# Last quad's down projection: two output blocks by token parts of 320 and 192, instead of one block by halves

## The chip, the core and the metric

The kernel runs on one core of one Trainium2 chip. The metric is the device time of one execution in microseconds (us): the median of 3 runs. Engines: TensorE (PE in the profile, PEld for its weight loads), VectorE (DVE), ScalarE (ACT), GpSimd (POOL) and SyncE (SP, which here only issues transfers).

## The reference

One block of a two-stream backbone over 512 latent tokens and 256 context tokens of width 2048: a mixing layer (gated linear attention and mLSTM heads), then a SwiGLU feed-forward layer with a depthwise 3x3 convolution on its gate branch, then the final norm. What the change touches is the end:

```python
h2 = rmsnorm(x, g_norm2) * (1 + sc2) + sh2
x = x + gt2 * conv_ffn(h2, rows, GRID_W, w_up, conv_w, conv_b, w_down)
...
return rmsnorm(x, g_final)
```

`conv_ffn` ends in a product of its 5504 hidden features with `w_down` (5504 x 2048). `rmsnorm` needs, for every token, the mean of the squares over all 2048 features, so no output of a token can be scaled before all 16 feature tiles of that token are done.

## The kernel before

**Layout.** Features lie on the 128 partitions and tokens along the free dimension. The residual stream is 16 tiles of 128 features x 512 tokens (`x2[k]`, tile name `xf` at the end). Matrix products are made in float32r, each operand split into a rounded part and its rest (`split`, L104: ScalarE casts, VectorE subtracts), and `mm3` (L120) issues three products per pair. Each product loads its own stationary weights.

**Stages.** Most of the time goes to the projections and the feed-forward layer. The hidden features are worked through in eleven quads (`QUADS`), each with `up_gate`, `convolve`, `up_val` and a down projection. The down projection of a quad has four output blocks of 512 features (four tiles each). For all quads but the last, `down_sums` adds each block to the residual stream in DRAM.

**The last quad** (L1339 to L1419) adds in SBUF instead. Blocks 0, 1 and 2 go through `down_block` (L1286): weights by `load_split`, then 48 products of 512 tokens into four PSUM banks (`dn`). Then, for each tile, VectorE adds the product to the residual (`residual`, L1084), ScalarE squares it by halves of 256 tokens (`square`, L1088; VectorE adds the squares up in `sqfq`), and ScalarE multiplies the tile by its column of g_final (L1365).

Block 3 is made by halves (`halves`, L1346) of 256 tokens, from weights that are split ahead of it (`dlh`, `dll`, L1369 to L1376), into banks `dl`. For each half, when its four tiles are done, `token_rstd` (L1104) makes the root: products of the squares with a column of ones give the sum per token (`ps_rmsf`), `mean_rsqrt` (L170) makes the root by two ScalarE and four VectorE steps (`rs_rmsf`), and products with the identity spread it over the partitions (`rb_rmsf`). `scaled` (L1377) then copies it for GpSimd (`r3s`), multiplies all 16 tiles of the half into output buffers (`o`, two tiles each), and issues eight transfers to DRAM per half. VectorE makes eleven of a half's 16 scalings and GpSimd five (L1389); tiles 12 to 15 take g_final in the same VectorE instruction (L1386).

**What sets the order.** While `pinned` is on (from L1395), TensorE keeps program order. The first half's sums are issued after the second half's first tile, its spread after the second tile, and its scalings then run on the other engines during the second half's last two tiles. The other engines' order is made by a scheduler at build time from data dependences and priorities (`tc.high_priority`); each engine then runs its list in order. PSUM has eight banks, `acc` and `psb` take them in turn.

Of the kernel before, what the change touches and what calls it, by code (L numbers as in the profile page):

```python
# [18 lines left out]
P = 128  # L19
# [4 lines left out]
T = 512  # L24
# [59 lines left out]
def block_kernel(ctx: ExitStack, tc: tile.TileContext, a: dict, out: bass.AP):  # L84
# [1019 lines left out]
    def token_rstd(sums, pl, name, n=T, idle=0):  # L1104

        nj = n // P
        ps = psb(f"ps_{name}", (P, nj))
        for i, sq in enumerate(sums):
            for j in range(nj):
                mm(ps[:, j : j + 1], sq[:, P * j : P * j + P], cst[:, C_ONE : C_ONE + 1],  # L1110
                   start=(i == 0 and j == 0), stop=(i == len(sums) - 1), skip_group_check=True)
        var, scr, r = (pl.tile([P, nj], F32, name=f"{t}_{name}", tag=t) for t in ("rs1", "rs2", "rs3"))
        with tc.high_priority():
            mean_rsqrt(ps, D, var, scr, r)
        yield
        o = psb(f"rb_{name}", (P, n))
        idle_products(o[:, 0:P], sums[0][:, 0:P], idle)
        for j in range(nj):
            mm(o[:, P * j : P * j + P], r[:, j : j + 1].to_broadcast([P, P]), ident, start=True, stop=True)
        yield o  # L1120
# [225 lines left out]
    halves = [slice(0, T // 2), slice(T // 2, T)]  # L1346
# [10 lines left out]
    for blk in range(3):  # L1357
        accs = down_block(q, blk)
        with tc.high_priority():
            for i in range(4):  # L1360
                residual(4 * blk + i, accs[i], modc[5])
        for k in range(4 * blk, 4 * blk + 4):
            for hf, sl in enumerate(halves):
                square(k, sums3[hf], sqp, f"fq{hf}", sl)
            S.activation(x2[k], x2[k], AF.Copy, scale=gnf[:, k : k + 1])  # L1365
        if blk == 0:
            for k in range(12, KT):
                nc.gpsimd.dma_start(x2[k], x2d[k])
    wd = []  # L1369
    for n, f in enumerate(fs):  # L1370
# [5 lines left out]
        wd.append((wh, wl))  # L1376
    def scaled(hf, sl, r3):  # L1377

        r3s = sqp.tile([P, T // 2], F32, name=f"r3s{hf}", tag=f"r3s{hf}")
        S.copy(r3s, r3)  # L1380
        for k in range(0, KT, 2):
            o = operand(k // 2, "l", "q", f"o{hf}_{k}", (P, 2, T // 2), F32)
            for i in range(2):
                xx = x2[k + i][:, sl]
                if k + i >= 12:
                    V.scalar_tensor_tensor(out=o[:, i, :], in0=xx, scalar=gnf[:, k + i : k + i + 1], in1=r3,  # L1386
                                           op0=ALU.mult, op1=ALU.mult)
                elif k in (2, 6) or k + i == 10:
# [3 lines left out]
            eng = nc.scalar if hf and k % 4 == 2 else nc.sync  # L1392
            eng.dma_start(out[k : k + 2, :, sl].rearrange("k p t -> p k t"), o)

    pinned[0] = True  # L1395
    root = None
    for hf, sl in enumerate(halves):
        accs = [acc(f"dl{hf}_{i}", (P, T // 2)) for i in range(4)]
        order = [(n, i) for n in range(len(fs)) for i in range(4)]
        if hf == 1:  # L1400
            order = [(n, i) for i in range(4) for n in range(len(fs))]
        for at, (n, i) in enumerate(order):
            if hf and at in (4, 8):
                with tc.high_priority():
                    r3 = next(root)
                    if at == 8:
                        scaled(0, halves[0], r3)
            gh, gl = gs[fs[n]]
            mm3(accs[i], wd[n][0][:, P * i : P * i + P], wd[n][1][:, P * i : P * i + P],
                gh[:, sl], gl[:, sl], n == 0, n == len(fs) - 1)  # L1410
        with tc.high_priority():
            for i in range(4):
                residual(12 + i, accs[i], modc[5], sl)
                square(12 + i, sums3[hf], sqp, f"fq{hf}", sl)
        root = token_rstd(sums3[hf], sqp, f"rmsf{hf}", T // 2, idle=4 * hf)
    with tc.high_priority():
        _, r3 = root
        scaled(1, halves[1], r3)
# [71 lines left out]
```

## Time and profile before

| | us |
|---|---|
| median of 3 runs | 2452.11 (2451.01 to 2452.73) |
| the profiled execution | 2453.06 |
| its span, first to last instruction | 2451.2 |
| TensorE busy | 2406.2 (98%) |
| VectorE busy | 1795.0 (73%) |
| ScalarE busy | 1003.7 (41%) |
| GpSimd busy | 176.5 (7%) |
| first product of block 2 | at 2412.57 |
| first product of block 3 | at 2423.45 |
| last product of block 3 ends its pace | at 2437.25 |
| second half's root spread over the partitions | at 2441.46 |

Times in the traces are us from the span's start. The profiled execution takes 1.86 us outside its span. The engines overlap, so busy shares don't add up; a stage is bound by what ends last in it, and the chain of waits follows that back from the last instruction. A matmul's duration in the rows includes the time in which its results drain from the array, beside the next one; the spacing of their starts is the pace.

### The profile page before, as it was taken

The numbers are of one execution on the slowest core, as the hardware profiler recorded it, in microseconds if no ns is written. First come the engines' busy times: TensorE is split into PE (matmuls) and PEld (weight loads), VectorE is DVE, ScalarE is ACT, GpSimd is POOL, SyncE is SP. The second block draws the span as 40 slices with busy tenths as digits, with TensorE's granted clock in tenths as the row PEclk, the third lists the DMA queues.
The fourth block names the chain that finished last, engine by engine and source line by source line (L and its number), as shares of the span: only waits on it lengthen the run. The fifth ranks groups of instructions, "written<-read, shape, count | busy, mean of one in ns | idle before, by whom it ended". The sixth has DMA issues, their size and how long they took to land.

```text
span 2451.2 us, 38648 instructions
## 1 busy us (share of the span) xinstructions
PE 2406.2 (98%) x15412; PEld 2170.5 (89%) x15412; DVE 1795.0 (73%) x2876; ACT 1003.7 (41%) x1494; POOL 176.5 (7%) x221
## 2 busy tenths in 40 slices
PE   6999999999999999999999999999999999999998
PEld 4887899899988888888998989999999999999997
DVE  6566856655456586769888787878787878787886
ACT  4225443222232242246544444444444444444445
POOL 0000000000000000000101010101111111111021
PEclk9999999999999999999999999999999999999999
DMA  9751111134355788843555455555555555546464
GB/s 383 286 173 55 46 44 52 61 112 129 129 181 187 245 301 283 282 148 112 126 144 143 130 139 137 136 140 129 139 135 140 128 145 124 147 123 148 117 185 133
DMA packets 122486, 373.65 MB, mean 152 GB/s; under 512 B 13912, under 2 KB 19010, under 8 KB 122306
## 3 DMA queue, kind: packets, MB, share of 16 engines
q1 hardware_dynamic: 95298, 318.75, 39.7%
q0 software_dynamic: 25920, 51.40, 11.6%
q8 instruction: 120, 1.97, 0.3%
q10 hardware_dynamic: 1088, 1.05, 0.1%
q14 instruction: 60, 0.49, 0.1%
HBM read 320.80 MB, written 50.34 MB: 151 GB/s over the span
## 4 chain that ended last, share of the span: by engine, by line
PE 88%; issue 6%; DVE 3%; DMA 2%; ACT 1%; POOL 0%; SPq 0%; DVEq 0%; POOLq 0%; ACTq 0%
PE a L111 19%; PE dn L111 17%; PE uv L111 16%; PE ug L111 15%; PE ga L111 7%; PE wo L111 7%; PE po L111 2%; PE ps_m L111 1%; PE sl L111 1%; DMA raw_m<-in_w_mod 1%; PE st L111 1%; PE cst L111 1%; DMA raw_uv<-in_w_up 0%; DVE ex L94 0%; DMA xl<-in_xT 0%
## 5 line engine op out<-in xcount | busy, mean ns | idle before, releaser
L111 PE MATMUL dn<-gh,lo_d 128*128 128x512 f32 x672 | 262.2, 390 | 1.6 <-DVE lo_d L106 1.6
L111 PE MATMUL dn<-gh,hi_d 128*128 128x512 f32 x672 | 261.6, 389 | 0.0
L111 PE MATMUL dn<-gl,hi_d 128*128 128x512 f32 x672 | 261.6, 389 | 0.0
L1257 DVE SCALAR_TENSOR_TENSOR cv<-pads,cwt,cv 128x512 f32<-128x512 f32 x344 | 239.3, 748 | 0.6
L1311 POOL DMA_DIRECT2D x2d<-st x160 | 140.1, 930 | 1143.5 <-ACT st L1310 1069.4
L106 DVE TENSOR_TENSOR lo_buv<-sum_uv,hi_buv 128x1024 fp32r<-128x1024 f32 x80 | 98.0, 1225 | 104.1 <-ACT hi_buv L105 101.4
L320 DVE SCALAR_TENSOR_TENSOR raw_m<-raw_m,crow 128x1024 f32<-128x1024 f32 x128 | 154.7, 1229 | 1.6 <-DMA raw_m<-in_w_mod 1.6
L111 PEld LDWEIGHTS dn<-gh,lo_d 128*128 128x128 f32 x672 | 126.1, 188 | 30.1 <-DVE lo_d L106 3.9
L111 PE MATMUL a<-hi_h,hTh 128*128 128x256 f32 x512 | 152.0, 297 | 0.5 <-ACT e L402 0.5
L111 PEld LDWEIGHTS dn<-gl,hi_d 128*128 128x128 f32 x672 | 126.2, 188 | 25.8
L111 PEld LDWEIGHTS dn<-gh,hi_d 128*128 128x128 f32 x672 | 126.2, 188 | 25.7
L111 PE MATMUL a<-lo_h,hTh 128*128 128x256 f32 x512 | 145.1, 283 | 0.0
L111 PE MATMUL a<-hi_h,hTl 128*128 128x256 f32 x512 | 144.9, 283 | 0.0
L105 ACT CAST hi_d<-raw_d 128x1024 fp32r<-128x1024 f32 x86 | 88.6, 1030 | 130.8 <-PE ug L111 70.6
L106 DVE TENSOR_TENSOR lo_d<-raw_d,hi_d 128x1024 fp32r<-128x1024 f32 x86 | 102.9, 1197 | 49.6 <-ACT hi_d L105 48.9
L111 PE MATMUL ug<-bth,hi_bug 128*128 128x256 f32 x480 | 136.8, 285 | 0.2 <-DVE t L1276 0.2
L111 PE MATMUL uv<-bth,lo_buv 128*128 128x256 f32 x480 | 135.9, 283 | 0.3 <-DVE lo_buv L106 0.3
L111 PE MATMUL ug<-bqh,lo_aug 128*128 128x256 f32 x480 | 135.8, 283 | 0.0
L111 PE MATMUL uv<-bqh,lo_auv 128*128 128x256 f32 x480 | 135.8, 283 | 0.0
L111 PE MATMUL uv<-bql,hi_auv 128*128 128x256 f32 x480 | 135.8, 283 | 0.0
L111 PE MATMUL ug<-bqh,hi_aug 128*128 128x256 f32 x480 | 135.8, 283 | 0.0
L111 PE MATMUL uv<-bth,hi_buv 128*128 128x256 f32 x480 | 135.8, 283 | 0.0
(410 smaller groups left out, 7255.4 us busy)
## 6 DMA issues: line engine op xcount, KB each, us to landing
raw_m<-in_w_mod SPq DMA_DIRECT2D x192, 512.0 KB, 5.2
raw_d<-in_w_down SPq DMA_DIRECT2D x82, 512.0 KB, 3.5
raw_ug<-in_w_up SPq DMA_DIRECT2D x80, 512.0 KB, 3.5
x2d<-st POOLq DMA_DIRECT2D x160, 256.0 KB, 5.5
raw_uv<-in_w_up SPq DMA_DIRECT2D x80, 512.0 KB, 5.7
raw_h<-in_w_heads SPq DMA_DIRECT2D x64, 512.0 KB, 3.5
raw_ga<-in_w_gates SPq DMA_DIRECT2D x32, 512.0 KB, 4.1
raw_wo<-in_w_out SPq DMA_DIRECT2D x32, 512.0 KB, 4.7
```

The lines of the kernel that those rows point to most:

```text
L105: cast[0] = S.copy(hi, x).ins
L106: return V.tensor_tensor(out=lo, in0=x, in1=hi.bitcast(F32), op=ALU.subtract).ins
L111: ins = PE.matmul(*args, **kw)
L320: V.scalar_tensor_tensor(out=x, in0=x, scalar=1.0, in1=crow[0], op0=ALU.mult, op1=ALU.mult, accum_out=mtot[:, at : at + 1])
L1257: V.scalar_tensor_tensor(out=t3, in0=src, scalar=w, in1=t3, op0=ALU.mult, op1=ALU.add)
L1311: nc.gpsimd.dma_start(x2d[k], t, accum_op=ALU.add)
```

## The change

- Blocks 2 and 3 of the last quad are both made by parts, and the parts are 320 and 192 tokens (`parts`) instead of halves of 256. Block 2 no longer goes through `down_block`; its weights are still loaded and split by `load_split` (two pairs of f, kept for both parts).
- A part runs block 2, then block 3. In the first part block 2 runs with f outermost, everything else with the output tile outermost. Each tile gets its residual and square as soon as it is done (`settle`), except in the first part's block 2, where all four follow at the end.
- The first part's sums are issued after the first tile of block 2 in the second part, its spread and its scalings after the third; `scaled` yields after each pair of tiles.
- `token_rstd` cuts a part into columns of 128 tokens, the last one moved back to end with the part: 0, 128 and 192 for 320 tokens, 0 and 64 for 192 tokens.
- Tiles 8 to 15 take g_final with the scaling on VectorE (before 12 to 15), so block 2 has no g_final step on ScalarE. GpSimd makes six scalings of the first part and four of the second. The tile pairs are scaled and written in the order 0, 8, 2, 10, 4, 12, 6, 14.

```diff
-    def token_rstd(sums, pl, name, n=T, idle=0):
+    def token_rstd(sums, pl, name, sl=slice(0, T), idle=0):
+        n = sl.stop - sl.start
+        cuts = [min(c, n - P) for c in range(0, n, P)]
+        ps = psb(f"ps_{name}", (P, len(cuts)))
...
-    halves = [slice(0, T // 2), slice(T // 2, T)]
+    parts = [slice(0, 320), slice(320, T)]
...
-    for blk in range(3):
+    for blk in range(2):
...
-    wd = []
+    wd = [[], []]
+    for n in range(0, len(fs), 2):
+        wh, wl = load_split(a["w_down"][2][:, fs[n] : fs[n] + 2, :], f"d{fs[n]}_2")
+        wd[0].extend((wh[:, i], wl[:, i]) for i in range(2))
...
-        for k in range(0, KT, 2):
-            o = operand(k // 2, "l", "q", f"o{hf}_{k}", (P, 2, T // 2), F32)
+        for at, k in enumerate((0, 8, 2, 10, 4, 12, 6, 14)):
+            o = operand(k // 2, "l", "q", f"o{hf}_{k}", (P, 2, n), F32)
             for i in range(2):
                 xx = x2[k + i][:, sl]
-                if k + i >= 12:
+                if k + i >= 8:
                     V.scalar_tensor_tensor(out=o[:, i, :], in0=xx, scalar=gnf[:, k + i : k + i + 1], in1=r3,
                                            op0=ALU.mult, op1=ALU.mult)
-                elif k in (2, 6) or k + i == 10:
+                elif k in (2, 6) or (k == 4 and hf == 0):
                     G.tensor_tensor(out=o[:, i, :], in0=xx, in1=r3s, op=ALU.mult)
                 else:
                     mul(o[:, i, :], xx, r3)
-            eng = nc.scalar if hf and k % 4 == 2 else nc.sync
+            eng = nc.scalar if hf and at % 2 else nc.sync
             eng.dma_start(out[k : k + 2, :, sl].rearrange("k p t -> p k t"), o)
+            yield
...
-    for hf, sl in enumerate(halves):
-        accs = [acc(f"dl{hf}_{i}", (P, T // 2)) for i in range(4)]
-        order = [(n, i) for n in range(len(fs)) for i in range(4)]
-        if hf == 1:
-            order = [(n, i) for i in range(4) for n in range(len(fs))]
-        for at, (n, i) in enumerate(order):
-            if hf and at in (4, 8):
-                with tc.high_priority():
-                    r3 = next(root)
-                    if at == 8:
-                        scaled(0, halves[0], r3)
...
-        with tc.high_priority():
-            for i in range(4):
-                residual(12 + i, accs[i], modc[5], sl)
-                square(12 + i, sums3[hf], sqp, f"fq{hf}", sl)
-        root = token_rstd(sums3[hf], sqp, f"rmsf{hf}", T // 2, idle=4 * hf)
+    for hf, sl in enumerate(parts):
+        for b, blk in enumerate((2, 3)):
+            accs = [acc(f"dl{hf}{blk}_{i}", (P, sl.stop - sl.start)) for i in range(4)]
+            by_f = hf == 0 and b == 0
+            order = [(n, i) for i in range(4) for n in range(len(fs))]
+            for n, i in sorted(order) if by_f else order:
+                if hf and b == 0 and n == 0 and i in (1, 3):
+                    with tc.high_priority():
+                        r3 = next(root)
+                        if i == 3:
+                            stores = scaled(0, parts[0], r3)
+                            for _ in range(3):
+                                next(stores)
+                gh, gl = gs[fs[n]]
+                wh, wl = wd[b][n]
+                mm3(accs[i], wh[:, P * i : P * i + P], wl[:, P * i : P * i + P],
+                    gh[:, sl], gl[:, sl], n == 0, n == len(fs) - 1)
+                if n == len(fs) - 1 and not by_f:
+                    settle(blk, i, accs[i], hf, sl)
+                    if hf and b:
+                        next(stores, None)
+            if by_f:
+                for i in range(4):
+                    settle(blk, i, accs[i], hf, sl)
+        root = token_rstd(sums3[hf], sqp, f"rmsf{hf}", sl, idle=4 * hf)
```

How the instructions stand after it is shown at three places. In the rows a tile's name has the program's buffer number behind it, and `xN` counts equal rows. The first is TensorE where the second half (now the second part) has finished its first output tile and the other half's sums follow; before:

```order
L111 MATMUL dl_0_23249<-gl_22756,dlh_23178 128x256
L111 MATMUL dl_0_23249<-gh_22755,dll_23179 128x256
L111 MATMUL ps_rmsf_23265<-cst,sqfq_22937 128x1 x2
L111 MATMUL ps_rmsf_23265<-cst,sqfq_23244 128x1 x2
L111 MATMUL ps_rmsf_23265<-cst,sqfq_23247 128x1 x2
L111 MATMUL dl_1_23250<-gh_22764,dlh_23160 128x256
```

and now, with `hi_d_2` and `lo_d_2` the split weights of block 2:

```order
L111 MATMUL dl_0_23233<-gl_22756,hi_d_2_23071 128x192
L111 MATMUL dl_0_23233<-gh_22755,lo_d_2_23072 128x192
L111 MATMUL ps_rmsf_23253<-cst,sqfq_22937 128x1 x3
L111 MATMUL ps_rmsf_23253<-cst,sqfq_23216 128x1 x3
L111 MATMUL ps_rmsf_23253<-cst,sqfq_23231 128x1 x3
L111 MATMUL dl_1_23234<-gh_22764,hi_d_2_23065 128x192
```

The products are 192 columns wide, there are nine sums instead of six (each is two instructions in a trace), and seven output tiles follow instead of three.

The second is VectorE from the first half's (part's) first scaling to the last residual (`xf<-dl`) of the second; before:

```order
L97 TENSOR_TENSOR o_0_23298<-xf_22849,rb_rmsf_23293 128x256 x2
L100 TENSOR_TENSOR sqfq_22939<-sqfq_22939,sqfq_23359 128x256
L1086 SCALAR_TENSOR_TENSOR xf_22856<-dl_2_23251,mod_66,xf_22856 128x256
L97 TENSOR_TENSOR o_4_23306<-xf_22851,rb_rmsf_23293 128x256 x2
L97 TENSOR_TENSOR o_8_23314<-xf_22853,rb_rmsf_23293 128x256
L1086 SCALAR_TENSOR_TENSOR xf_22856<-dl_3_23252,mod_66,xf_22856 128x256
```

and now (`dl_3_23236` is the last tile of block 2, the four after it are block 3), in two pieces that follow each other, the scalings first:

```order
L97 TENSOR_TENSOR o_0_23310<-xf_22849,rb_rmsf_23304 128x320 x2
L1396 SCALAR_TENSOR_TENSOR o_8_23314<-xf_22853,cols,rb_rmsf_23304 128x320 x2
L1396 SCALAR_TENSOR_TENSOR o_10_23358<-xf_22854,cols,rb_rmsf_23304 128x320 x2
L1396 SCALAR_TENSOR_TENSOR o_12_23397<-xf_22855,cols,rb_rmsf_23304 128x320
L1086 SCALAR_TENSOR_TENSOR xf_22854<-dl_3_23236,mod_66,xf_22854 128x192
L1396 SCALAR_TENSOR_TENSOR o_12_23397<-xf_22855,cols,rb_rmsf_23304 128x320
L1396 SCALAR_TENSOR_TENSOR o_14_23420<-xf_22856,cols,rb_rmsf_23304 128x320 x2
```

Then the additions and residuals of the second part, up to the first step of its root:

```order
L100 TENSOR_TENSOR sqfq_22939<-sqfq_22939,sqfq_23335 128x192
L1086 SCALAR_TENSOR_TENSOR xf_22855<-dl_0_23338,mod_66,xf_22855 128x192
L100 TENSOR_TENSOR sqfq_22939<-sqfq_22939,sqfq_23355 128x192
L1086 SCALAR_TENSOR_TENSOR xf_22855<-dl_1_23339,mod_66,xf_22855 128x192
L100 TENSOR_TENSOR sqfq_22939<-sqfq_22939,sqfq_23375 128x192
L1086 SCALAR_TENSOR_TENSOR xf_22856<-dl_2_23340,mod_66,xf_22856 128x192
L1086 SCALAR_TENSOR_TENSOR xf_22856<-dl_3_23341,mod_66,xf_22856 128x192
L173 TENSOR_SCALAR rs_rmsf_23431<-ps_rmsf_23424 128x2
```

All ten of VectorE's first-part scalings now stand ahead of block 3's residuals; before, six of eleven stood behind the last residual, among and behind the steps of the second root.

The third is SP's list of output transfers in the second half, before:

```order
L1393 DMA out<-o_14_23326 128x2x256
L1393 DMA out<-o_0_23393 128x2x256
L1393 DMA out<-o_4_23401 128x2x256
L1393 DMA out<-o_8_23409 128x2x256
L1393 DMA out<-o_12_23417 128x2x256
```

and now:

```order
L1403 DMA out<-o_6_23416 128x2x320
L1403 DMA out<-o_2_23457 128x2x192
L1403 DMA out<-o_0_23449 128x2x192
L1403 DMA out<-o_6_23473 128x2x192
L1403 DMA out<-o_4_23465 128x2x192
```

The other four of each half stand in ScalarE's list: 2, 6, 10, 14 before; 8, 10, 12, 14 now. The first of the second part on SP is a pair that GpSimd scales, where it was a pair of VectorE's.

37 lines of the change are left out of this document (21 added, 16 removed).

## The prediction

> **What bounds the kernel now.** I read the page first, for the engine that carries the time.
>
> ```profile
> span 2451.2 us, 38648 instructions
> PE 2406.2 (98%) x15412; PEld 2170.5 (89%) x15412; DVE 1795.0 (73%) x2876; ACT 1003.7 (41%) x1494; POOL 176.5 (7%) x221
> PE 88%; issue 6%; DVE 3%; DMA 2%; ACT 1%; POOL 0%; SPq 0%; DVEq 0%; POOLq 0%; ACTq 0%
> ```
>
> TensorE (PE) is busy 98% of the span and is 88% of the chain of waits. The change touches only the end of the program, so what counts is which wait ends last there. I cut the end into stages with the windows view: the third output block (2412.57 on), the fourth by its first half, the second half with the first half's norm, the second half's norm, and the outputs. The columns are start and end, length, then busy us and instructions per engine, clock, DMA share and GB/s.
>
> ```profile
> 2412.57:2423.45 10.88, 10.88 (x49) 9.01 (x48) 8.65 (x19) 8.43 (x18) 0.00 (x0) 1.00 0.01 2
> 2423.45:2429.21 5.76, 5.76 (x50) 5.75 (x48) 3.27 (x9) 3.14 (x7) 0.00 (x0) 1.00 0.00 0
> 2429.21:2437.25 8.04, 7.95 (x67) 7.66 (x65) 5.71 (x18) 3.08 (x10) 2.22 (x3) 1.00 0.00 0
> 2437.25:2441.46 4.21, 3.26 (x26) 2.80 (x24) 3.37 (x12) 0.88 (x3) 1.48 (x3) 1.00 0.99 345
> 2441.46:2451.20 9.74, 0.00 (x1) 0.00 (x0) 3.97 (x11) 0.37 (x1) 3.46 (x5) 0.72 0.81 282
> ```
>
> Up to 2437.25 TensorE is full. Then come 4.21 us for the norm of the second half and 9.74 us for its outputs. The chain of waits (start, length, engine, tile, line) shows the order of that tail.
>
> ```profile
> 2437.48 0.46 DVE xf L1086
> 2437.97 0.42 ACT sqfq L1093
> 2438.44 0.62 PE ps_rmsf L111 x4
> 2440.54 0.17 DVE rs_rmsf L177
> 2440.75 0.72 PE rb_rmsf L111 x4
> 2441.50 0.38 ACT r3s L1380
> 2441.90 1.36 DVE o L97 x4
> ```
>
> Last residual, its square, the token sums, the root, its spread over the partitions (rb_rmsf, done at 2441.46; I call this moment R), then the output scalings. Whether scalings or transfers end last is told by the DMA view of 2436.5 to 2451.2, in 40 slices of 0.3675 us.
>
> ```profile
> GB/s 0 0 0 329 379 379 387 376 382 385 379 387 368 387 371 376 385 373 50 267 373 360 390 382 385 385 376 390 376 387 385 379 390 387 123 8 0 0 0 0
> ```
>
> Two bursts at about 380 GB/s: from 2437.6 to 2443.2 for the first half, from 2443.6 to 2449.2 for the second. So each half's 2.1 MB costs 5.6 us, the outputs' end is set by bandwidth once R has come, and from R to the last byte it takes 7.7 us (2.1 until data flow, 5.6 of data), then 2.0 to the span's end. The first half has drained 0.4 us before the second starts.
>
> **The change, part by part.** The sum runs against the profiled execution (2453.06 us, of which 2451.2 is the span). The three runs shown have their median 0.95 below it, at 2452.11, and I carry the sum over to that.
>
> *TensorE.* The 48 products of 512 columns and 96 of 256 become 96 of 320 and 96 of 192. These rows give mean ns of one, pipeline drain included, and one group of weight loads.
>
> ```profile
> L111 PE MATMUL dn<-gh,hi_d 128*128 128x512 f32 x672 | 261.6, 389 | 0.0
> L111 PE MATMUL a<-hi_h,hcl 128*128 128x384 f32 x256 | 86.3, 337 | 0.0
> L111 PE MATMUL dl<-gl,dlh 128*128 128x256 f32 x32 | 9.1, 283 | 0.0
> L111 PE MATMUL po<-v,ed 128*128 128x258 f32 x64 | 19.1, 380 | 0.0
> 2430.89 1.42 PEld L111 LDWEIGHTS ps_rmsf<-cst,sqfq 128*128 128x128 f32 x12 [0.29 <-DVE sqfq L100]
> 2432.43 0.26 ACT L172 ACTIVATE rs_rmsf<-ps_rmsf,eps 128x2 f32<-128x2 f32 x1 [1.66 <-PE ps_rmsf L111]
> 2433.61 0.15 DVE L177 SCALAR_TENSOR_TENSOR rs_rmsf<-rs_rmsf,rs_rmsf 128x2 f32<-128x2 f32 x1
> ```
>
> The stage of 5.76 us holds 48 products of 256 columns, 0.120 us each; its mean of 283 ns is thus 163 ns of drain over the pace. Less 163, 512 and 384 columns go at 226 and 174 ns. The line through the three is 0.415 ns a column, so 320 columns cost 0.147 us. For 192 the line says 0.093, but no row shows a float32r product below 256 columns, and another row bounds it: the token sums, of one column each, load new weights for every instruction, and their 12 loads take 1.42 us, (1.42 - 0.19) / 11 = 0.112 us apart. Every product here loads weights too, so I take 0.112.
>
> [...]
>
> From 2412.57: first part 96 x 0.147 = 14.1, to 2426.7. Second part 96 x 0.112 = 10.75. Its sums now have three columns, 18 instructions x 0.112 = 2.0, and the spread 6 x 0.112 = 0.7. TensorE's last product starts its drain at **2440.1 instead of 2437.25, 2.9 us later**: 2.45 from the products (before 10.88 + 96 x 0.120 = 22.4 us, now 24.85), 0.65 from the sums, 0.2 from the spread, less 0.4 of small waits in the old stages, which the longer products cover.
>
> *VectorE.* Steps of each kind:
>
> ```profile
> 2411.84 1.40 DVE L1086 SCALAR_TENSOR_TENSOR xf<-dn,mod,xf 128x512 f32<-128x512 f32 x2
> 2414.49 1.22 DVE L106 TENSOR_TENSOR lo_d<-raw_d,hi_d 128x1024 fp32r<-128x1024 f32 x1
> 2428.33 1.27 DVE L1086 SCALAR_TENSOR_TENSOR xf<-dl,mod,xf 128x256 f32<-128x256 f32 x3 [2.30 <-PE dl L111]
> 2441.90 2.41 DVE L97 TENSOR_TENSOR o<-xf,rb_rmsf 128x256 f32<-128x256 f32 x7 [0.82 <-ACT r3s L1380]
> 2444.23 1.65 DVE L1386 SCALAR_TENSOR_TENSOR o<-xf,cols,rb_rmsf 128x256 f32<-128x256 f32 x4
> 2429.63 1.15 ACT L1093 ACTIVATE sqfq<-xf 128x256 f32<-128x256 f32 x3 [0.36 <-DVE xf L1086]
> 2442.00 3.46 POOL L1389 TENSOR_TENSOR o<-xf,r3s 128x256 f32<-128x256 f32 x5 [3.27 <-ACT r3s L1380]
> 2436.69 8.80 SPq L1393 DMA_DIRECT2D out<-o  x12
> ```
>
> At 256 columns a residual steps by 0.40 us, a plain scaling or an addition by 0.33, a scaling with g_final (L1386) by 0.39, a square by 0.37 (0.42 alone), GpSimd's by 0.69; the residual of 512 (0.70 in the mean) puts a column near 1.1 ns. So 320 columns cost 0.46, 0.40, 0.46 for the first three and 192 cost 0.33, 0.27, 0.33; GpSimd's 192 cost 0.52, by ratio.
>
> The first part's R comes after the third product group of the second part: 2426.7 + 36 x 0.112 + 2.0 = 2432.7, spread 0.9 with its drain, copy r3s 0.45 (0.38 at 256 columns): scalings start at 2434.1. The order rows put seven scalings (2 x 0.40 + 5 x 0.46 = 3.1) ahead of the residual dl_3 of block 2 in the second part: 2437.2, whose product was ready at 2434.9. Then that residual, three scalings and an addition (0.33 + 1.4 + 0.27): 2439.2. Then, twice, residual, square, addition in a row, because the addition stands ahead of the next residual: 0.41 + 0.36 + 0.27 and two hops of 0.035 make 1.1 each: 2441.4. Then two residuals, 0.33 + 0.41: **the last ends at 2442.15; TensorE had its product ready at 2440.3**. What is queued behind is all of the second part's norm.
>
> From the last residual's end (2437.94) to R took 3.5 us before. Between the root's first and last step lay 1.6 us there (2439.06 to 2440.71), with scalings between; for the first half 1.33 (2432.43 to 2433.76), with one addition between. The new order has nothing between: I take 1.0, hence 2.9 us, and R at 2445.05, **3.6 us later**.
>
> *Outputs.* 192 of 512 tokens are 1.57 MB, 4.1 us at 380 GB/s instead of 5.6. SP's first transfer of that part waits for two GpSimd scalings: 0.04 + 0.31 + 0.04 + 2 x 0.52 = 1.4 us after R, and 0.9 from issue to data (2436.69 to 2437.6): 2.3 instead of 2.1. VectorE's twelve (4 x 0.27 + 8 x 0.33 = 3.7) end earlier than the bandwidth does. R to the last byte: 6.4 instead of 7.7, **1.3 less**. The first part's 2.62 MB (6.9 us) start at about 2436.9 and drain by 2443.8, before the second part's data at 2447.4, so they hide, with 3.6 us to spare.
>
> *Costed at nothing.* Block 2 no longer gets its g_final scaling on ScalarE, which is off the path. The weights come by the same transfers in the same order. The second pair's low halves are ready at 2414.49 + 1.22 = 2415.7 and now wanted after 26 x 0.147, at 2416.4: 0.7 us of cover; late splits would cost TensorE what they exceed it by. Banks and o buffers are released well ahead by these times.
>
> **Sum:** +3.6 - 1.3 = **+2.3 us**: 2455.4 for the profiled execution, 2454.4 for the median, 0.09% more.
>
> Bounds for the unknown price. Below: 0.093 a product saves 60 x 0.019 = 1.1 us after R of the first part and 0.7 before it on TensorE, but VectorE, which is late, gets only the 0.7: +1.6 us. Above: the plain float32 product of 258 columns takes two instructions of 380 - 163 = 217 ns, 0.84 ns a column each, so 192 columns would cost 2 x 0.161 = 0.323 us; that is the first rival.
>
> **The rivals.**
> Slower: *narrow products lose float32r's pace.* All float32r rows have 256 columns or more, so nothing shows that the pace holds at 192; the two prices of one operand size (0.120 and 2 x 0.217) show that the same bytes can take the dear path. At 0.323 the second part costs 31.0 instead of 10.75, TensorE ends at 2460.4, VectorE is then on time, R comes at 2460.4 + 0.2 + 0.4 + 2.9 = 2463.9: +22.4 - 1.3 = +21.1, or 2473.2. It speaks against it that a float32r product is one pass at each of three widths. It passes 0.2% (4.9 us, about what a measurement of this kernel can tell from no change) from about 0.155 us a product. A half-way pace, 0.173, would give some +7, 2459.
>
> VectorE keeps up: if its steps overlap better than I add them, R follows TensorE's end: 2440.3 + 0.4 + 2.9 = 2443.6, so +2.1 - 1.3 = +0.8: 2453; with 0.093 a product, 2451. For it: small steps that I took singly; against: the order is fixed.
>
> Narrower rows transfer worse: rows of 768 bytes instead of 1024; if the second part still took 5.6 us, +3.8: 2456. No row shows 768.
>
> **How the numbers follow.** My forecast gets 0.38, VectorE keeping up 0.10, the poorer transfers 0.05, the lost pace 0.41, half-way 0.04, a gain of more than 4.9 us 0.02: it would need a third of the 14 us after TensorE's last product. Faster 0.02, within 0.2% 0.53, slower 0.45. The likeliest case alone spans 2452.0 to 2456.5. As the slower case holds 0.41, the range reaches over it: 2451.5 to 2475.5. The predicted time is that of the likeliest, 2454.4.
>
> **What would show it.** The spacing of the 192-column products: 0.112 or so, 0.093, or 0.3. The last residual about 1.8 us after its product is ready. R at 2445, the second burst of some 4.1 us with an idle gap of about 3 us ahead of it, and no output of the first part in flight at R. I am wrong if the products are dearer than 0.155, or if the last residual waits for TensorE.

## The result

The changed kernel takes 2459.15 us (median of 20 runs, 2454.6 to 2463.57); the kernel before, run beside it, 2453.70 (20 runs, 2450.66 to 2456.86). The ratio is **1.0023, 95% interval 1.0016 to 1.0030**: slower by 0.23%, some 5.5 us, where I forecast 2.3. 1.6 us of the distance in absolute time is the base: the three runs that I had of the kernel before are among these 20 and lie below their median.

The profiled execution took 2458.75 us. The head of its page:

```profile
span 2457.0 us, 38761 instructions
PE 2411.9 (98%) x15468; PEld 2178.2 (89%) x15468; DVE 1796.3 (73%) x2880; ACT 1001.3 (41%) x1490; POOL 176.5 (7%) x221
```

Nothing shows there: 5.8 us of span is too little for shares. So again the end in stages (start and end, length, busy us and count of PE, PEld, DVE, ACT and POOL, granted clock, DMA share, GB/s): the first part of both blocks, the second part up to the first part's spread (cut where the clock changes), the rest of the second part, TensorE's wait, the second part's norm, the outputs.

```profile
2413.04:2427.10 14.06, 14.06 (x97) 14.05 (x96) 11.36 (x25) 8.57 (x18) 0.00 (x0) 1.00 0.01 2
2427.10:2431.80 4.70, 4.70 (x45) 4.70 (x43) 2.10 (x8) 1.52 (x5) 0.00 (x0) 1.00 0.00 0
2431.80:2435.20 3.40, 3.40 (x19) 3.40 (x18) 1.19 (x3) 0.57 (x2) 0.00 (x0) 0.51 0.00 0
2435.20:2442.02 6.82, 6.82 (x63) 6.82 (x62) 6.01 (x14) 1.12 (x4) 5.05 (x6) 0.99 0.51 185
2442.02:2443.83 1.81, 0.27 (x3) 0.09 (x2) 1.10 (x4) 0.55 (x2) 0.00 (x0) 1.00 1.07 394
2443.83:2448.36 4.53, 4.38 (x24) 4.00 (x24) 1.24 (x6) 1.15 (x4) 0.00 (x0) 0.69 0.40 148
2448.36:2457.00 8.64, 0.00 (x0) 0.00 (x0) 3.74 (x12) 0.32 (x1) 2.23 (x4) 0.70 0.54 182
```

The column to read is the clock. In the kernel before it was 1.00 in every stage up to R. Here it is **0.51 from 2431.80 to 2435.20**, where 19 instructions of TensorE take the time of some 30 at 0.112 us, and **0.69 in the second part's norm**. TensorE is "busy" in the first of the two from end to end, so the busy share can't show it.

The chain of waits (start, length, engine, tile, line):

```profile
2428.60 1.92 PE ps_rmsf L111 x18
2430.52 3.92 PE dl L111 x24
2434.45 1.17 PE rb_rmsf L111 x6
2435.64 0.44 ACT r3s L1390
...
2436.99 2.29 DVE o L1396 x5
2439.28 0.33 DVE xf L1086
2439.61 1.37 DVE o L1396 x3
...
2443.78 0.34 DVE xf L1086
...
2444.55 1.05 PE ps_rmsf L111 x8
2445.61 2.73 PE rb_rmsf L111 x12
2448.36 0.33 ACT r3s L1390
```

24 products of 192 columns take 3.92 us instead of 24 x 0.112 = 2.7. Then scalings run ahead of block 2's last residual, as forecast (the five of L1396 are shown, two stand before them), and VectorE is the chain until the last residual. And in the second part's norm the spread stands with 12 instructions, 2.73 us, where the kernel before has four, 0.72: the eight idle products ahead of the spread, 0.21 us each at half clock, outlast the root and so come into the chain. On the engines' timeline (start, length, engine, line) the root's last step, the idle products (`rb_rmsf<-sqfq,cst`) and the spread proper (`rb_rmsf<-cst,rs_rmsf`) show it:

```profile
2446.56 0.16 DVE L177 SCALAR_TENSOR_TENSOR rs_rmsf<-rs_rmsf,rs_rmsf 128x2 f32<-128x2 f32 x1
2445.47 2.00 PE L111 MATMUL rb_rmsf<-sqfq,cst 128*128 128x128 f32 x8
2447.26 1.06 PE L111 MATMUL rb_rmsf<-cst,rs_rmsf 128*128 128x128 f32 x4
```

The root is done at 2446.72, the spread starts 0.5 us later, behind the idle products, and takes 1.06 us.

The groups of products by shape (count, then busy us and mean ns of one, drain included; block 2's name their weights hi_d or lo_d, block 3's dlh or dll):

```profile
L111 PE MATMUL dl<-gh,hi_d 128*128 128x192 f32 x16 | 5.0, 310 | 0.0
L111 PE MATMUL dl<-gh,dll 128*128 128x320 f32 x16 | 4.9, 309 | 0.0
L111 PE MATMUL dl<-gh,dll 128*128 128x192 f32 x16 | 4.4, 274 | 0.0
```

Less the 163 ns of drain, 320 columns go at 146 ns and 192 at 111, block 3's; block 2's 192 columns hold the half-clock ones and so average 310.

The outputs, GB/s in 40 slices of 0.5125 us from 2436.5 to 2457:

```profile
GB/s 0 16 0 0 165 377 392 395 395 395 397 382 395 395 392 397 392 247 0 0 0 0 0 0 0 0 0 0 328 354 369 369 369 369 367 370 175 0 0 0
```

The first part drains by 2445.7, hidden. The second part's rows of 768 bytes go at 369, not 395; on 1.57 MB that is 0.3 us against the first part's pace and 0.1 against the 380 of my sum.

### The profile page after: what moved, and what is told of

Its sections match the earlier page's. It is cut to its first block, busy times and chain, and to the rows that moved or that the text cites. A ratio compares the mean times of both kernels' runs of the same rounds, so it can differ in the third digit from the quotient of the medians.

```text
span 2457.0 us, 38761 instructions
## 1 busy us (share of the span) xinstructions
PE 2411.9 (98%) x15468; PEld 2178.2 (89%) x15468; DVE 1796.3 (73%) x2880; ACT 1001.3 (41%) x1490; POOL 176.5 (7%) x221
## 4 chain that ended last, share of the span: by engine, by line
PE 87%; issue 6%; DVE 3%; DMA 2%; ACT 1%; POOL 0%; SPq 0%; DVEq 0%; POOLq 0%; ACTq 0%
PE a L111 19%; PE uv L111 16%; PE dn L111 16%; PE ug L111 15%; PE ga L111 7%; PE wo L111 7%; PE po L111 2%; PE ps_m L111 1%; PE sl L111 1%; PE dl L111 1%; DMA raw_m<-in_w_mod 1%; PE st L111 1%; PE cst L111 1%; DVE cv L1258 0%; DMA xl<-in_xT 0%
## 5 line engine op out<-in xcount | busy, mean ns | idle before, releaser
L111 PE MATMUL dn<-gh,lo_d 128*128 128x512 f32 x656 | 256.1, 390 | 2.0 <-DVE lo_d L106 2.0
L111 PE MATMUL dn<-gh,hi_d 128*128 128x512 f32 x656 | 255.5, 389 | 0.0
L111 PE MATMUL dn<-gl,hi_d 128*128 128x512 f32 x656 | 255.5, 389 | 0.0
L111 PE MATMUL ug<-btl,hi_bug 128*128 128x256 f32 x480 | 135.9, 283 | 0.0
```

The costliest lines, as they stand in the source:

```text
L111: ins = PE.matmul(*args, **kw)
```

## The experiments

Two theories stood after this. **Clock**: the half-clock stretches are the missing time, and they come because the array is hardly fed there (18 one-column sums beside narrow products; TensorE's wait for VectorE at the end). **Queue**: VectorE's fixed order is the missing time. All times are beside runs of the kernel before (their median was 2453.6 to 2454.2 in the three sessions). A ratio is not the quotient of the medians, as executions of one kernel scatter over 5 to 10 us; one hundredth of a per cent is 0.25 us.

To compare profiled executions I take every moment against the first product of the two blocks, because what lies ahead differs from execution to execution by several us and is not the change's. For the kernel before, it is the first product of block 2, 2412.57. R is the start of the copy r3s. Each row but the forecast is one execution.

| profiled execution | last product starts | last residual ends | R | end of span |
|---|---|---|---|---|
| kernel before | 24.56 | 25.37 | 28.93 | 38.63 |
| forecast | 27.5 | 29.6 | 32.5 | 40.9 |
| changed | 28.97 | 31.39 | 35.32 | 43.99 |
| changed, once more | 27.34 | 29.83 | 34.14 | 42.82 |
| sums of 128 columns | 27.34 | 29.82 | 34.04 | 42.73 |
| the same and fill | 27.48 | 29.96 | 33.17 | 41.84 |
| two blocks, equal halves | 25.99 | 27.07 | 30.11 | 40.34 |
| the widths alone | 28.12 | 30.74 | 35.01 | 43.07 |
| VectorE's order, first try | 27.79 | 30.17 | 34.43 | 43.10 |
| VectorE's order, second try | 27.84 | 29.21 | 33.27 | 41.96 |
| all three | 27.34 | 28.67 | 31.92 | 40.59 |

### Two blocks, equal halves

```diff
-    parts = [slice(0, 320), slice(320, T)]
+    parts = [slice(0, 256), slice(256, T)]
```

> The changed kernel with both parts 256 tokens wide: the two blocks by parts stay, the widths of 320 and 192 go. The profiled execution of the changed kernel had R at 2448.3 us and 13 narrow products at about 0.213 us, in a stretch in which the granted clock was 0.52 to 0.61 (2431.8 to 2435.2). The clock theory (18 one-column sums and narrow products, and TensorE's wait at the end, make the throttle halve the clock for 3.4 us at a time, which cost some 2.8 us beyond my sum): 12 sums and products of 0.120 us keep TensorE better filled, so no stretch under 0.9 before the last product, R near 2442 to 2444, 7.7 from R to the last byte as in the kernel before, time 2453 to 2456. The queue theory (VectorE's fixed order, ten scalings of the first part ahead of the last block's residuals, makes R late whatever the widths): the last residual still ends more than 1.3 us after its product, and R is past 2444, time 2456 to 2458.

Measured: 2454.71 us (11 runs), ratio 1.0003, interval 0.9994 to 1.0012. The stage of its norm, from the last product to R, and the one wait ahead of it:

```profile
2435.30:2439.40 4.10, 3.37 (x27) 2.91 (x25) 2.10 (x8) 0.89 (x4) 0.00 (x0) 1.00 0.50 177
```

```profile
2413.63 0.38 PE L111 MATMUL dl<-gh,lo_d 128*128 128x256 f32 x1 [1.07 <-DVE lo_d L106]
```

Clock 1.00 up to R, and 4.10 us for the norm as in the kernel before. The last residual is 0.8 us late, not 1.3. So **two blocks by parts cost nothing that the runs can tell; the widths of 320 and 192 do**. In the profiled execution the span still ends 1.7 us later against the first product than in the kernel before (40.34 against 38.63), and the second row accounts for 1.07 of it. It is the cover of 0.7 us for the second pair's low halves that the prediction named: it is gone in this execution, and TensorE waits 1.07 us for VectorE's split. A kernel without that wait wasn't tried.

### The widths alone

The kernel before, its last block by 320 and 192 tokens (with the changed kernel's `token_rstd`, which cuts a part of 320 into three):

```diff
-    halves = [slice(0, T // 2), slice(T // 2, T)]
+    halves = [slice(0, 320), slice(320, T)]
```

> The kernel before, its last block alone by parts of 320 and 192 tokens instead of halves: the widths without the two blocks. TensorE: 48 x 0.147 and 48 x 0.112 against 96 x 0.120 (+0.9), 18 sums against 12 (+0.7), 6 spreads against 4 (+0.2 with the first part): last product 1.7 us later; outputs 1.1 less after R. Without the clock +0.6: 2454.3. The clock theory: the same 18 one-column sums beside products of 0.112 us stand here as in the changed kernel, 2 us with hardly a column, so in the executions in which they lie in one stretch of the raster a half-clock stretch of 1.6 us follows: 2454.3 to 2455.9, and VectorE, with one residual per 1.3 us, is not late. If the widths are harmless and the two blocks carry the cost, it is the time of the kernel before.

Measured: 2457.47 us (11 runs), ratio 1.0019, interval 1.0010 to 1.0028: nearly all of the change's loss without its two blocks, and more than either number that I had set down. Its stages around the sums and in the second norm, and its chain:

```profile
2428.30:2431.76 3.46, 3.39 (x30) 3.39 (x30) 1.12 (x7) 0.72 (x3) 0.00 (x0) 1.00 0.00 0
2431.76:2435.17 3.41, 3.41 (x17) 3.34 (x17) 1.99 (x6) 0.79 (x2) 1.12 (x2) 0.50 0.00 0
...
2438.58:2443.40 4.82, 3.73 (x18) 3.54 (x17) 1.42 (x6) 0.83 (x3) 0.00 (x0) 0.50 1.03 374
```

```profile
2428.37 2.17 PE ps_rmsf L111 x18
...
2434.00 2.87 DVE o L97 x7
```

The 18 sums lie in the stretch that ends at 2431.76; the next 3.41 us are at 0.50, and so is the second norm. And VectorE is late here too (2.87 us of scalings in a row; the last residual ends 2.35 us after its product, 0.8 with equal halves), which I had excluded: its lateness comes mostly with the widths, not with the second block.

### VectorE's order, first try

Residuals, additions and the first part's scalings kept in the order in which the code writes them:

```diff
-        V.scalar_tensor_tensor(out=xx, in0=ps, scalar=gate[:, k : k + 1], in1=xx, op0=ALU.mult, op1=ALU.add)
+        return V.scalar_tensor_tensor(out=xx, in0=ps, scalar=gate[:, k : k + 1], in1=xx, op0=ALU.mult, op1=ALU.add)
...
+            tail(residual(k, ps, modc[5], sl))
+            while adds:
+                adds.pop(0)()
```

> The changed kernel with one thing else: on VectorE the second part's residuals and additions and the first part's scalings stand in the order in which the code writes them, four scalings ahead of block 2's last residual and six more spread between the following ones, the last two behind the last residual. In the changed kernel the last residual ended about 2.1 us after its product was ready. The queue theory: it ends 0.6 us or less after its product, so R comes 1.5 to 1.8 us earlier, near 2446.6, and the time falls by 1.5 to 1.8 us, to about 2457.3. The clock theory: TensorE's stretch at half clock near 2432 stays, since nothing ahead of it changes; the gain is that of the queue and no more, unless TensorE's shorter wait at the end (1.5 us in the changed kernel) also spares the second drop, then up to 1 us more. A theory by which VectorE's order costs nothing expects 0.

Measured: 2456.79 us (11 runs), ratio 1.0012, interval 1.0003 to 1.0020. The time is as the queue theory had it; the mechanism isn't. In its chain

```profile
2440.05 0.91 DVE o L1421 x2
2440.96 0.34 DVE xf L1086
...
2442.75 2.78 PE rb_rmsf L111 x12
```

two scalings still stand ahead of the last residual, which ends 2.1 us after its product, as before. Against the first product R comes at 34.4, with a wait of 0.5 us for weights in it that the unchanged kernel doesn't have; without it R would be 0.2 us earlier than the 34.1 of that kernel's second execution. What its profile lacks beside the changed kernel's first one is the half-clock stretch near the sums: the 24 products behind them take 2.77 us instead of 3.92.

### VectorE's order, second try

Against the first try:

```diff
-            while adds:
+            while adds and k != 13:
                 adds.pop(0)()
...
-            if blk == 3:
-                next(stores, None)
+            for _ in range({11: 1, 13: 2}.get(k, 0)):
+                next(stores)
...
-                if blk == 3:
-                    adds.pop(0)()
```

> The changed kernel with VectorE's tail in an order of its own: of the first part's ten scalings four stand ahead of block 2's last residual, two behind it, two between the last block's second and third residual, two behind the last one; each addition stands a residual later, so that none waits for its own square. No sums or products are changed. The queue theory: the last residual ends at most 0.8 us after its product instead of 2.1 to 2.5, so R comes 1.5 us earlier and the time falls by 1.5 to 2, to 2457.3. The clock theory adds: with TensorE waiting 0.6 us or less there, the low stretch behind the last product is as short as in the kernel before (4 us), and the drop at the end goes too in most executions: 2.5 to 3 less in all, 2456.3; the drop near the first part's sums comes or goes with the raster, 1.6 us.

Measured: 2457.71 us (11 runs), ratio 1.0017, interval 1.0008 to 1.0026. The last residual now ends 1.1 us after its product (I had said 0.8), and R comes 0.9 us earlier than in the changed kernel's second execution, although TensorE loses 0.5 us to a wait for weights. But the chain behind it

```profile
2438.21 0.33 DVE xf L1086
...
2440.85 2.78 PE rb_rmsf L111 x12
```

still has the 12 instructions at half clock (0.72 in the mean from 2438.20 to 2443.65). I had expected a shorter wait to spare that stretch in most executions; in this one it didn't.

### Fewer sums

The first part's squares 14 and 15 are added on VectorE, so 6 sums stand on TensorE instead of 18:

```diff
-        if first or k >= KT - 2:
+        if first or (k >= KT - 2 and tag != "fq0"):
```

> The changed kernel with the first part's last two squares added to the running total on VectorE, so that its token sums are 6 instructions of TensorE instead of 18, and two additions of 320 columns are new on VectorE ahead of them. Without any clock effect: 12 x 0.112 = 1.3 us less on TensorE, less up to 0.3 for the two additions, so R of the first part 1 us earlier and everything behind it too: about 1 us less, 2458.1. The clock theory: with the row of thin instructions cut to a third the clock stays at 1.00 from 2424 to 2440, the 13 narrow products at half pace and the dear spread go (1.7 us more), and the time falls by 2.7, to about 2456.4. If the drop comes from the narrow products alone, it stays, and the gain is 1.

Measured: 2458.76 us (9 runs), ratio 1.0023, interval 1.0013 to 1.0032: no gain, a miss for both numbers. The sums now wait for VectorE's additions, and the clock halves all the same:

```profile
2433.69 0.83 PE L111 MATMUL ps_rmsf<-cst,sqfq 128*128 128x1 f32 x6 [1.39 <-DVE sqfq L100]
```

```profile
2435.60:2439.00 3.40, 3.40 (x19) 3.40 (x18) 1.24 (x5) 0.36 (x1) 0.00 (x0) 0.50 0.00 0
```

Here 1.39 us of waiting and 0.83 us of sums were followed by a clock of 0.50, as 1.92 us of sums were by 0.51 in the changed kernel.

### The same sums, 128 columns wide

```diff
-                mm(ps[:, j : j + 1], sq[:, c : c + P], cst[:, C_ONE : C_ONE + 1],
+                mm(wide[:, w * j : w * j + w], sq[:, c : c + P], ones[:, 0:w],
```

> The changed kernel with the token sums of both parts done with 128 columns of ones instead of one column (128 equal sums, of which one is read): as many instructions, as many weight loads, at the same 0.112 us or so, only more columns through the array. By the sum of instruction times this changes nothing, or adds the drain of 127 columns, 0.05 us, once per part: 2459.2. The clock theory in its form 'the throttle follows what the array does, not whether TensorE has an instruction': the stretch at 0.52 to 0.61 near 2432 goes, R of the first part 0.6 earlier, 13 products 0.1 us cheaper each: up to 1.9 less, 2457.3. If the clock still halves at the same place, its cause isn't the one-column sums.

Measured: 2457.35 us (11 runs), ratio 1.0014, interval 1.0005 to 1.0023. Its stages from the first part's sums on, and its second norm:

```profile
2432.40:2437.84 5.44, 5.44 (x51) 5.44 (x50) 2.61 (x10) 1.66 (x5) 0.00 (x0) 1.00 0.00 0
...
2446.40:2451.22 4.82, 4.78 (x24) 4.45 (x24) 1.24 (x6) 1.16 (x5) 0.00 (x0) 0.65 0.38 140
```

No half clock near the sums, as the clock theory had it; the end's stretch stays. One execution doesn't prove it, as the last experiment shows: the sums may also miss the half clock by where they fall in time.

### The same, and a fill for the wait

```diff
+        if idle and n < T:
+            idle_products(psb(f"pre_{name}", (P, P)), ident, 8)
```

> The changed kernel with token sums of 128 columns (as in the run before it) and eight 128-column products without use (16 instructions, 1.8 us at 0.112) between the last product and the second part's sums, where TensorE otherwise waits 1.8 us for VectorE. VectorE's work and order stay. The clock theory in the form that the earlier traces suggest (the clock is set for stretches of 3.41 us on a fixed raster whose place differs from execution to execution, and is halved in the stretch after one in which the array was fed under about a third of the time): no stretch at half clock between the first part's sums and R, the last residual to R 2.9 us instead of 3.9 to 4.2, so 1 to 1.3 us less than with the 128-column sums alone and 2.5 to 3 less than the changed kernel: 2456.2. The queue theory: nothing waits for TensorE there, so the time is that of the 128-column sums alone, 2457.4, or later where the fill outlasts the wait.

Measured: 2455.19 us (11 runs), ratio 1.0011, interval 1.0002 to 1.0020. From the sums to the last product, and from there to R:

```profile
2427.85:2441.26 13.41, 13.41 (x122) 13.41 (x121) 10.02 (x27) 3.73 (x11) 5.04 (x6) 1.00 0.25 92
2441.26:2443.87 2.61, 2.60 (x23) 2.41 (x21) 1.70 (x5) 1.04 (x4) 0.00 (x0) 1.00 1.06 392
2443.87:2446.95 3.08, 2.76 (x20) 2.38 (x20) 0.64 (x4) 0.74 (x3) 0.00 (x0) 1.00 0.35 128
```

The clock is 1.00 in all three. VectorE's work is untouched and the last residual as late as ever (2.2 us), yet it is 3.2 us from there to R instead of 3.9 to 4.3. **Useless products shorten this tail**, by 0.9 us against the 128-column sums alone; the queue theory has no place for that. The medians can't show it: the ratios of the two versions, 1.0011 and 1.0014, have intervals that overlap nearly whole.

### All three

The second order, sums of 128 columns, and a fill of four products.

> The changed kernel with all that helped: VectorE's order of its own, token sums of 128 columns, and four 128-column products without use (8 instructions, 0.9 us) in the shorter wait that is left. No half-clock stretch before R if the fill is enough, the last residual 0.8 us after its product, from the last residual to R 2.9. By its steps R is 1.5 (queue) + 1.1 (end stretch) us earlier than in the changed kernel, and 1.6 more where that had its other stretch: 2.6 to 4.2 less, 2455.0 to 2456.5. If queue and clock are one effect seen twice, it comes out no better than the fill alone, 1.0011 of the kernel before.

Measured: 2454.63 us (11 runs), ratio 1.0006, interval 0.9997 to 1.0014. From the last residual's end to R:

```profile
2441.78:2445.03 3.25, 2.93 (x24) 2.55 (x23) 1.55 (x6) 0.83 (x4) 0.00 (x0) 1.00 1.04 379
```

R comes 2.2 us earlier than in the changed kernel's second execution and 3.4 earlier than in its first; the order alone gave 0.9 and the fill alone 1.0 against the second. In these single executions order and clock add; the ratios point the same way, with intervals that overlap. No version here is measurably faster than the kernel before.

### Thin and dense instructions in the kernel before

24 instructions without use behind the first half's sums, of one column:

```diff
+        if idle == 0 and n < T:
+            extra = psb(f"extra_{name}", (P, P))
+            for _ in range(12):
+                mm(extra[:, 0:1], ident, cst[:, C_ONE : C_ONE + 1], start=True, stop=True)
```

> The kernel before with 24 one-column instructions without use (twelve products of a plain float32 identity and a column of ones) behind the first half's token sums, in the middle of the last block. They load new weights each, so TensorE is occupied all the time. Without the clock: 24 x 0.112 = 2.7 us more, all in front of the last product, so R and the time +2.7: 2456.9. The clock theory: together with the 12 sums that is 4 us in which hardly a column goes through the array, longer than a stretch of the raster (3.41), so in every execution a half-clock stretch follows, 1.7 us more, in some two: +4.4 or more, 2458.5 to 2460, and the profile shows a stretch at 0.5 near 2436.

and of 128 columns, `mm(extra, ident, ident, ...)`:

> As the run before it, with 128 columns in each of the 24 instructions instead of one (identity by identity). The same weight loads at the same pace, 0.112 us. Both theories: +2.7 us, 2456.9. The clock theory: no half-clock stretch before the last product, so this is 1.7 us or more below the run with one column. If the two come out alike, how full the array is doesn't matter to the clock.

Measured: thin 2460.13 us (11 runs), ratio 1.0018, interval 1.0009 to 1.0027; dense 2455.64 us (11 runs), ratio 1.0006, interval 0.9997 to 1.0015. The thin kernel's chain and the stage behind its extra instructions:

```profile
2435.99 2.68 PE extra_rmsf L111 x24
2438.67 2.41 PE dl L111 x12
```

```profile
2438.98:2442.39 3.41, 3.41 (x19) 3.41 (x18) 0.50 (x2) 0.42 (x2) 0.00 (x0) 0.50 0.02 5
```

The dense kernel's:

```profile
2433.29 2.79 PE extra_rmsf L111 x24
2436.08 1.43 PE dl L111 x12
```

```profile
2437.35:2440.55 3.20, 3.20 (x30) 3.20 (x29) 2.64 (x8) 1.11 (x3) 2.10 (x3) 1.00 0.03 5
```

The extra instructions take nearly the same time, 2.68 and 2.79 us, and TensorE is busy in both. Behind the thin ones 12 products of 256 columns take 2.41 us, behind the dense ones 1.43. **In these two executions the clock followed how much went through the array, not whether TensorE had an instruction.**

The raster of 3.41 us lies differently in the two executions. All 24 thin instructions fall into one stretch, while a border near 2434.3 (an estimate: three stretches of 3.413 us ahead of 2444.5, within the last spread) cuts the dense ones after the tenth. Cut in the same way, the thin ones would leave some 1,300 columns in the stretch before the border, where the dense kernel has 2,570; that is an estimate from the trace. The two ratios point the same way, with intervals that overlap.

From block 3's first product to the span's end the kernel before takes 27.7 us, the dense one 30.3 (2.5 more; 2.7 were set down), the thin one 31.6 (3.9 more; at least 4.4 were set down, 2.7 without a clock effect). From the same moment to the last product's start it is 17.7 us against the dense kernel's 16.2, 1.5 more. At the span's end it is 1.3 more, because the dense execution has, by an estimate from its last spread, a half-clock stretch of its own at the end of the second norm: that spread takes 0.95 us in the chain instead of 0.72.

### The changed kernel once more

> The changed kernel once more, unchanged, for the raster: if the halving near the first part's sums hangs on where the raster of 3.41 us falls, another execution has it at another place or not at all, and its last product starts 1.6 us earlier against the first product of the two blocks; if it is a fixed property of the program, it comes at the same place with the same length. The stretch at the end should come in nearly every execution, since TensorE's low time there is 6 us, longer than a stretch.

Measured: 2458.74 us (10 runs), ratio 1.0020, interval 1.0011 to 1.0029; profiled at 2456.41. The token sums alone, counted in stretches of 3.41 us, in the first execution (two stretches) and in the second (three) (PE busy and count first; the clock behind ACT's):

```profile
2428.39:2431.80 3.41, 2.09 (x18) 2.05 (x18) 0.16 (x1) 0.26 (x1) 1.00 0.00 0
2431.80:2435.21 3.41, 0.00 (x0) 0.00 (x0) 0.00 (x0) 0.00 (x0) 0.51 0.00 0
```

```profile
2425.33:2428.74 3.41, 1.47 (x14) 1.56 (x14) 0.00 (x0) 0.00 (x0) 1.00 0.00 0
2428.74:2432.15 3.41, 0.62 (x6) 0.53 (x5) 0.16 (x1) 0.26 (x1) 1.00 0.00 0
2432.15:2435.57 3.42, 0.00 (x0) 0.00 (x0) 0.00 (x0) 0.00 (x0) 1.00 0.03 7
```

A raster is a fixed grid in time. Its borders are laid by each execution's own half-clock stretches, whose starts lay whole multiples of 3.413 us apart in the first execution (2431.88, 2445.53 and 2452.36 are 13.65 and 6.83 us apart, 4 and 2 x 3.413; 1083.62 and 2431.88 are 1348.26 us apart, which is 395 x 3.4133; the views cut at 2431.80). In the first all 18 sums fall into one stretch, and the next is at half clock (0.51). In the second the border cuts them, and there is no drop: the last product starts 1.63 us earlier against the first. The sums are at the same place of the program in both. Counted in columns, of which some 8,200 would fit into a stretch (an estimate: 3.41 us at the 0.415 ns a column of the prediction's line), the first execution's stretch with the sums holds 2,513, the second's two hold 3,598 and 4,868. The two versions with VectorE's own order agree: there too the border cuts the sums, no stretch ahead of the one in which the products end holds fewer than 3,850, and none is at half clock. So in these executions the drop at the sums was a matter of where the raster fell, as expected, and the end's stretch came again (0.63 in the second norm).

The execution of all three above shows the wider sums with the raster in a bad place. All 18 sums lie in one of its stretches too; counted alone again, in it and in the next:

```profile
2427.49:2430.91 3.42, 2.19 (x18) 2.09 (x18) 0.00 (x0) 0.18 (x1) 1.00 0.00 0
2430.91:2434.32 3.41, 0.00 (x0) 0.00 (x0) 0.16 (x1) 0.08 (x1) 1.00 0.00 0
```

With 128 columns each the stretch holds 4,800 columns instead of 2,513, and the next stays at full clock (1.00 instead of 0.51). VectorE's order differs too, but only behind the sums. So with all 18 sums in one stretch in both executions, their columns are what tells the two apart.

An instruction on TensorE was not enough to keep the clock up: the first execution's stretch with the sums, 2428.39 to 2431.80, was busy from end to end (3.41 of 3.41 us, 33 instructions), and the next was at 0.51.

## Why the prediction was right and wrong

**Pace of the products: right.** 0.147 and 0.112 us were forecast, 0.146 and 0.111 stand in the groups. The rival that float32r's pace is lost at 192 columns is out. I had given it 0.41, more than the 0.38 of my own forecast, though I called that one the likeliest. The range reached to 2475.5 for the rival's sake and held the time for the wrong reason, by luck: 2459.15 lies above the 2456.5 at which my likeliest case ended, and the loss of 0.23% beyond the 0.2% within which I had put 0.53.

**Last product 2.9 us later: right at full clock, wrong in the first profiled execution.** Forecast 27.5 after the first product; 27.34 in the second execution, 28.97 in the first. The 1.63 us between them are the half-clock stretch (0.51 for 3.40 us; at full clock in the second).

**VectorE late: right.** The last residual was to end 1.85 us after its product is ready; it ends 2.2 after. The order, the seven scalings and the additions ahead of each next residual are as put. "VectorE keeps up" is out.

**"From the last residual to R I take 2.9": the step that failed,** with the products' pace taken at full clock throughout. It is 3.9 and 4.3 us in the two executions of the changed kernel, 3.2 where a fill keeps the clock up; the 0.3 between 3.2 and 2.9 is not the clock's, and no run takes it apart. The sum had no term for the clock, though the view of the stages had a column for it and showed 0.72 at the very end of the kernel before. The sum had none for the eight idle products either. Before, they lay beside the root and cost nothing; at 0.21 us each they outlast it by 0.5 us.

**Outputs: right but for 0.3 us.** From R to the span's end 8.4 was forecast, 8.64 measured. "Narrower rows transfer worse" is true in direction (395, 380 and 369 GB/s for rows of 1280, 1024 and 768 bytes) and costs 0.1 us against my 380, where I gave that rival 1.5. The first part's transfers hide, with a gap of 5.3 us.

**The sum.** Of the first execution's 43.99 us, 3.1 are beyond the forecast: 1.4 up to the last product, 0.4 to the last residual, 1.0 to R, 0.3 behind it. By the comparisons above the clock costs 1.6 us up to the last product, where the forecast at full clock was 0.2 too late, and 0.7 on the way to R. 0.5 more lie ahead of the two blocks, where the first product comes at 2413.04 instead of 2412.57. The fully mended kernel, all three, ends at 40.6, about the forecast, but with an order that saves some 1.2 us (40.59 against the 41.84 of the fill alone) which the forecast had counted as lost.

Shown: that the widths and not the two blocks carry most of the cost; in single profiled executions, that a stretch in which the array was hardly fed was followed by one at half clock, with thin instructions (0.51 in the changed kernel, 0.50 behind the 24 thin ones) and with a wait (0.50 with fewer sums, where TensorE waited 1.39 us); and, by such executions too, that the two half-clock stretches and VectorE's order are separate costs and add. Open: whether there is a threshold and where, and whether columns are quite what counts; the third of the time that the expectation of the fill has was an estimate (2,513 of some 8,200 are 0.31). A stretch of 2,513 columns (the changed kernel) and one of 2,816 (TensorE's wait at the end, with 128-column sums) were followed by half clock, one of 2,572 (the dense kernel) was not. Open too: in what share of executions the drop near the sums comes, since only profiled ones show it.

## What to carry to other kernels

When a change makes TensorE's instructions narrower or leaves it waiting in a tail, read the clock column of the stages, not the busy share, and give the clock a term: here a stretch of 3.40 us at 0.51 cost 1.6 us (half its length, 1.7, by an estimate from these two numbers), and whether it came depended on where the raster fell. The thin helper products here, 18 one-column sums, were cheap by the row (1.92 us) and dear by what followed them in the first execution; with 128 columns they took 2.03 us and the clock was 1.00 behind them. Idle products that hide a latency must be priced at half clock too: here 0.21 us each, against 0.113 at full clock (0.91 us for the eight of the fill in all three).

## What the runs showed that I had not expected

- Eight useless 128-column products in a wait, together with wider sums, made the changed kernel's tail 1.0 us shorter than in its second execution and 2.2 shorter than in its first; the ratios to the kernel before, 1.0011 against 1.0023, agree, though their intervals overlap.
- One-column instructions at 0.112 us and 128-column ones at 0.116 (2.68 and 2.79 us for 24) take nearly the same time, and the first had a clock of 0.50 behind them, the second 1.00.
- Executions reach the last quad's end at times that differ by several us: the first product of the two blocks comes at 2411.88 and 2413.04 in the changed kernel, and at 2409.29 to 2417.18 in its variants, which hardly differ from it up to there. Comparing tails from there on told more than the medians.
